# Low parts of weight pieces by GpSimd's accumulating DMA in an encoder's mixers

## The chip, the cores and the metric

The kernel runs on one core of a Trainium2 chip. The metric is the device time of one execution in microseconds (us); the median of three runs of the kernel before is 834.88 us (833.3 to 836.93). Five engines run side by side, each in the order of its own instructions: TensorE (PE) multiplies, VectorE (DVE) and ScalarE (ACT) work on tiles, GpSimd (POOL) does small work, and SyncE (SP) issues DMA transfers. They wait for each other by semaphores.

## The reference

Two layers of an encoder block for 256 tokens of 1,024 float32 values. In each layer, three branches (mLSTM, Fourier, S5) are computed from one projection, gated and summed, and a squared-ReLU MLP follows:

```python
for l in range(DEPTH):
    h = rmsnorm(x, g_mix_pre[l])
    z = h @ w_in[l] + b_in[l]                       # q, k, v, o, gates of the cells, Fourier, S5, 3 x 1024 gates
    y_m = mlstm_branch(z[q, k, v, o, ig, fg]) @ w_up_mlstm[l]
    y_f = fourier_branch(z[fourier]) @ w_up_fourier[l]
    y_s = s5_branch(z[s5], ...)
    gates = sigmoid(z[gates])
    mixed = gates[0] * y_m + gates[1] * y_f + gates[2] * y_s
    x = x + rmsnorm(mixed @ w_out[l], g_mix_post[l])
    f = square(relu(rmsnorm(x, g_ffn_pre[l]) @ w_ffn1[l])) @ w_ffn2[l]
    x = x + rmsnorm(f, g_ffn_post[l])
```

## The kernel before

Every large product is made in three matmuls of a shorter float format (float32r). A weight W and the activations h are each split into a high and a low part, and PE adds hi·hi, hi·lo and lo·hi into a PSUM bank (`mm3`, lines 261 to 264). The split of the activations, `hhi` and `hlo`, is done once per layer.

The weights come in pieces. A piece of the mixers' pairs is 512 rows by 256 columns of the weight (512 KB), as a tile of 128 partitions by 4 row blocks by 256 columns. `wload` (lines 190 to 205) makes it ready in three steps: SP loads `raw` from device memory (L200), ACT rounds it to `hi` (tile `whi`, L202), and DVE subtracts, lo = raw - hi (tile `wlo`, L204). There are 5 raw tiles, 4 `whi` and 4 `wlo` tiles; a step waits until the tile that it writes is free.

`wstat_pair` (lines 323 to 335) makes 256 output columns for all tokens as two halves of one PSUM bank. It takes two pieces one after the other, and for each piece 2 halves x 4 row blocks x 3 = 24 matmuls of 256 columns, with the weights as the stationary operand. ACT then evicts the two halves, to the q and k tile `qk` (L1043) or through a tanh for the gates (L1062). In one mixer the pairs come in this order: one for S5, four for q and k, two for the output gate o, four for branch gate 1 and four for gate 2; the four of gate 0 come later, among the up-projections.

Between the pieces, `tick(budget)` takes steps from two side queues, in which the convolutions, the mLSTM cells, the Fourier branch and the S5 branch are written as generators. What finally sets the order on each engine is a list scheduler that plays the program through with costs of its own when it is built; the kernel gives it the program order, the buffers and a few fixed orders. So an edit in one place can move instructions elsewhere.

Two side steps matter below. The stabilisers of the cells (`stabilisers`) write a small tile to device memory (`md`), read it back as a broadcast of 1,024 KB into the ring tile `Gm` (L856, by SP), and then POOL runs four selects on it (L870). The ring tile is free only after PE has read the S5 tables that lay in it (L685). And at the end of the mixer, `cell_norm` (POOL L957 and L958, ACT L964) scales the heads `hm`, `cell_out` transposes them on PE (L188, tiles acc from hm), and DVE and ACT make the operand `ym` (L974, L976) of the mLSTM up-projection.

POOL issues no DMA in this kernel.

Of the kernel before, what the change touches and what calls it, by code (L numbers as in the profile page):

```python
# [10 lines left out]
F32 = mybir.dt.float32  # L11
F32R = mybir.dt.float32r
AF = mybir.ActivationFunctionType
ALU = mybir.AluOpType

P = 128
D = 1024
# [3 lines left out]
NK = D // P  # L21
# [12 lines left out]
OFF_Q = 0  # L34
# [6 lines left out]
OFF_GATE = OFF_S5 + M_S5  # L41
# [77 lines left out]
def encoder_kernel(ctx: ExitStack, tc: tile.TileContext, a: dict, out: bass.AP):  # L119
# [67 lines left out]
    def transpose(o, i, k=P):  # L187
        nc.tensor.transpose(o, i, cst[:k, C_ID:C_ID + k])  # L188

    def wload(pieces, shape, in_ring=None):  # L190

        raw = wp.tile(shape, F32, tag="raw", name=nm("raw"))
        if in_ring:
            both = ring(in_ring, [P, 2] + shape[1:], F32R)
            hi, lo = both[:, 0], both[:, 1]
        else:
            hi = wp.tile(shape, F32R, tag="whi", name=nm("whi"), bufs=TAIL)
            lo = wp.tile(shape, F32R, tag="wlo", name=nm("wlo"), bufs=TAIL)
        for dst, src in pieces:
            nc.sync.dma_start(dst(raw), src)  # L200
        yield
        act(hi, raw, AF.Copy)  # L202
        yield
        latest[0] = V.tensor_sub(lo, raw, hi.bitcast(F32)).ins  # L204
        return hi, lo
# [7 lines left out]
    def pieces_of(w, k0, kn, c0, cn):  # L213
        return ([(lambda r: r, w[k0 * P:(k0 + kn) * P, c0:c0 + cn].rearrange("(k p) c -> p k c", p=P))], [P, kn, cn])

    def now(gen):

        while True:
            try:
                next(gen)  # L220
            except StopIteration as e:
                return e.value
# [29 lines left out]
            while self.at[2] < len(self.specs):  # L252
                self.lo()

    def wunit(pieces, shape, in_ring=None):
        return now(wload(pieces, shape, in_ring))

    def wcols(w, k0, kn, c0, cn, in_ring=None):
        return wunit(*pieces_of(w, k0, kn, c0, cn), in_ring)

    def mm3(o, lhi, llo, rhi, rlo, start, stop):
        mm(o, lhi, rhi, start=start, stop=False)  # L262
        mm(o, lhi, rlo, start=False, stop=False)  # L263
        mm(o, llo, rhi, start=False, stop=stop)  # L264
# [55 lines left out]
        while side[which]:  # L320
            tick(1.0)

    def wstat_pair(w, c0, nk, ahi, alo, kper=4, budget=0.0):


        bank = mm_ps()
        ps = [bank[:, c * S:(c + 1) * S] for c in range(2)]
        for k0 in range(0, nk, kper):
            hi, lo = wcols(w, k0, kper, c0, 2 * P)
            for c in range(2):  # L330
                for k in range(kper):
                    mm3(ps[c], hi[:, k, c * P:(c + 1) * P], lo[:, k, c * P:(c + 1) * P],
                        ahi[:, k0 + k, :], alo[:, k0 + k, :], k0 + k + c == 0, k0 + k + c == nk)
            tick(budget)
        return bank

    def rstd_of(ss):
# [654 lines left out]
    def mixer(l, iu, vu, after):  # L992
# [44 lines left out]
            side[1].append(s5_branch(l, U, yg))  # L1037
        side[0] += [stabilisers(l, zf, st), fourier(zf, fo_y)][::-1 if l == 0 else 1]
        for nq, c2 in enumerate((1, 3, 0, 2)):
            ps = wstat_pair(w, OFF_Q + c2 * 2 * P, NK, hhi, hlo, budget=B)  # L1040
            for c in range(2):
                i = c2 * 2 + c
                act(qk[:, i, :], ps[:, c * S:(c + 1) * S], AF.Identity, bias=col(l, "qkb", i))  # L1043
                side[0].append(conv_silu(l, qk, i))
            if nq % 2:
                for h in range(2 * (c2 % 2), 2 * (c2 % 2) + 2):
                    side[0].append(cells(l, qk, st, h))
# [8 lines left out]


        def gate_pair(g, c2, dst, budget):
            ps = wstat_pair(w, OFF_GATE + g * D + c2 * 2 * P, NK, hhi, hlo, budget=budget)
            for c in range(2):  # L1060
                i = c2 * 2 + c
                act(dst(i), ps[:, c * S:(c + 1) * S], AF.Tanh, scale=0.5, bias=col(l, "gb", g * 8 + i, half=True))  # L1062
# [281 lines left out]
```

## Time and profile before

| | |
|---|---|
| median of three runs | 834.88 us (833.3 to 836.93) |
| the profiled execution | 834.29 us, its span 831.6 us |
| PE busy | 810.7 us (97%) |
| DVE busy | 597.6 us (72%) |
| ACT busy | 472.4 us (57%) |
| POOL busy | 30.3 us (4%) |
| DMA | 147.87 MB, 178 GB/s in the mean; one hardware queue holds nearly all of it |

The profile is of one execution. Its span goes from the first to the last instruction; the execution's time is 2.7 us more. Busy time of PE counts a matmul as long as it is in the array, and matmuls overlap, so the distance of two starts says more than a duration. An engine's idle time costs only where another engine is waiting for it.

### The profile page before, as it was taken

How to read it: one execution, taken by the hardware profiler on the slowest of the kernel's cores; microseconds unless marked ns; L12 is line 12 of the kernel's file. 1: busy time of each engine (PE TensorE's matmuls, PEld its weight loads, DVE VectorE, ACT ScalarE, POOL GpSimd, SP SyncE). 2: the span in 40 equal slices, each digit the busy share in tenths (PEclk: the TensorE clock that was granted, in tenths of full speed). 3: DMA queues.
4: the chain of work that ended last, by engine and by line, in shares of the span. 5: the costliest groups of instructions: out<-in, count | busy, mean ns of one | idle time of the engine just before them, and what ended most of it. 6: DMA issues, size and time to landing. Idle time of an engine off the chain costs nothing.

```text
span 831.6 us, 14910 instructions
## 1 busy us (share of the span) xinstructions
PE 810.7 (97%) x5825; PEld 749.4 (90%) x5825; DVE 597.6 (72%) x1071; ACT 472.4 (57%) x784; POOL 30.3 (4%) x51
## 2 busy tenths in 40 slices
PE   7999999998999999999999999999999999999996
PEld 5899999998878999999879999999997899999995
DVE  5898899887685567667568798776876755555563
ACT  4668764586464458467654355666865444444451
POOL 1000200000020000000010010000000100000000
PEclk9999999999999999999999999999999999999999
DMA  8785843554755564765837554555666555566651
GB/s 264 222 229 142 247 121 103 152 177 148 257 138 179 185 188 137 235 186 186 271 96 229 152 179 128 152 178 153 176 185 215 181 158 193 185 186 195 181 174 50
DMA packets 122262, 147.87 MB, mean 178 GB/s; under 512 B 22310, under 2 KB 104398, under 8 KB 121936
## 3 DMA queue, kind: packets, MB, share of 16 engines
q1 hardware_dynamic: 122044, 146.66, 57.9%
q8 instruction: 45, 0.74, 0.4%
q10 hardware_dynamic: 148, 0.27, 0.1%
q14 instruction: 25, 0.20, 0.1%
HBM read 144.33 MB, written 2.57 MB: 177 GB/s over the span
## 4 chain that ended last, share of the span: by engine, by line
PE 71%; DVE 2%; ACT 1%; issue 1%; POOL 1%; DVEq 0%; POOLq 0%; ACTq 0%
PE mm L262 12%; PE mm L264 12%; PE mm L263 12%; PE acc L263 8%; PE acc L264 8%; PE acc L262 8%; PE mm L279 2%; PE mm L278 2%; PE mm L295 1%; PE mm L188 1%; PE mm L281 1%; PE acc L743 1%; PE acc L939 1%; DVE wlo L204 1%; DVE x_sb L386 0%
## 5 line engine op out<-in xcount | busy, mean ns | idle before, releaser
L204 DVE TENSOR_TENSOR wlo<-raw,whi 128x1024 fp32r<-128x1024 f32 (+1 forms) x237 | 287.6, 1215 | 153.1 <-ACT whi L202 152.1
L202 ACT ACTIVATE whi<-raw 128x1024 fp32r<-128x1024 f32 (+1 forms) x237 | 248.5, 1052 | 241.3 <-PE mm L263 141.6
L262 PE MATMUL mm<-hT,whi 128*128 128x256 f32 x1024 | 290.9, 284 | 0.0
L264 PE MATMUL mm<-hT,wlo 128*128 128x256 f32 x1024 | 290.4, 284 | 0.0
L263 PE MATMUL mm<-hT,whi 128*128 128x256 f32 x1024 | 290.2, 283 | 0.0
L262 PEld LDWEIGHTS mm<-hT,whi 128*128 128x128 f32 x1024 | 192.8, 188 | 1.5
L263 PEld LDWEIGHTS mm<-hT,whi 128*128 128x128 f32 x1024 | 192.9, 188 | 1.1
L264 PEld LDWEIGHTS mm<-hT,wlo 128*128 128x128 f32 x1024 | 193.3, 189 | 0.2
L263 PE MATMUL acc<-wlo,ringB 128*128 128x512 f32 x280 | 109.3, 392 | 0.7 <-DVE wlo L204 0.7
L264 PE MATMUL acc<-whi,ringB 128*128 128x512 f32 x280 | 108.8, 391 | 0.0
L262 PE MATMUL acc<-whi,ringB 128*128 128x512 f32 x280 | 106.2, 390 | 0.0
L263 PEld LDWEIGHTS acc<-wlo,ringB 128*128 128x128 f32 x280 | 52.6, 188 | 12.1 <-DVE wlo L204 1.9
L264 PEld LDWEIGHTS acc<-whi,ringB 128*128 128x128 f32 x280 | 52.6, 188 | 11.0
L262 PEld LDWEIGHTS acc<-whi,ringB 128*128 128x128 f32 x280 | 52.6, 188 | 10.2
L279 PE MATMUL mm<-whi,hT 128*128 128x512 f32 (+1 forms) x84 | 30.3, 369 | 1.9 <-DVE hT L371 1.8
L906 DVE SCALAR_TENSOR_TENSOR t1k<-ringB,pc,t1k 128x254 f32<-128x254 f32 (+1 forms) x64 | 31.0, 484 | 0.9
L278 PE MATMUL mm<-whi,hT 128*128 128x512 f32 (+1 forms) x84 | 30.5, 373 | 0.7 <-ACT whi L202 0.5
L262 PE MATMUL mm<-ringB,whi 128*128 128x256 f32 x96 | 27.4, 286 | 1.7 <-ACT ringB L976 1.7
L380 DVE SCALAR_TENSOR_TENSOR w2k<-acc,ringA 128x512 f32<-128x512 f32 x16 | 10.6, 688 | 24.7 <-ACT t1k L378 24.7
L263 PE MATMUL mm<-ringB,whi 128*128 128x256 f32 x96 | 27.3, 285 | 0.0
L264 PE MATMUL mm<-ringB,wlo 128*128 128x256 f32 x96 | 27.2, 284 | 0.0
L378 ACT ACTIVATE t1k<-acc 128x512 bf16<-128x512 f32 x16 | 9.5, 595 | 30.4 <-PE acc L264 30.4
(334 smaller groups left out, 1156.8 us busy)
## 6 DMA issues: line engine op xcount, KB each, us to landing
raw<-in_w_ffn_dram SPq DMA_DIRECT2D x128, 512.0 KB
raw<-in_w_in_dram SPq DMA_DIRECT2D x84, 512.0 KB
raw<-in_w_out_dram SPq DMA_DIRECT2D x16, 512.0 KB
raw<-in_w_glu_dram SPq DMA_DIRECT2D x16, 256.0 KB
raw<-in_w_up_mlstm_dram SPq DMA_DIRECT2D x8, 512.0 KB
ringB<-md SPq DMA_DIRECT2D x2, 1024.0 KB
raw<-in_w_up_fourier_dram SPq DMA_DIRECT2D x4, 512.0 KB
raw<-in_w_in_dram SPq DMA_DIRECT2D x4, 408.0 KB
```

The source lines that it names most:

```text
L188: nc.tensor.transpose(o, i, cst[:k, C_ID:C_ID + k])
L202: act(hi, raw, AF.Copy)
L204: latest[0] = V.tensor_sub(lo, raw, hi.bitcast(F32)).ins
L262: mm(o, lhi, rhi, start=start, stop=False)
L263: mm(o, lhi, rlo, start=False, stop=False)
L264: mm(o, llo, rhi, start=False, stop=stop)
L278: mm(o, hhi[:, k, tt], hi, start=k == 0, stop=False)
L279: mm(o, hlo[:, k, tt], hi, start=False, stop=False)
L281: mm(o, hhi[:, k, tt], lo, start=False, stop=k == NK - 1)
L378: act(junk(), ps[c], AF.Square, accum_out=ss[:, c:c + 1])
L380: stt(f, ps[c], ROOT_D, gpost[:, half(c)], ALU.mult, ALU.mult)
L906: stt(u[:, lo_:hi_], z[:, lo_ + o:hi_ + o], col(l, "cw", j * 8 + i), u[:, lo_:hi_], ALU.mult, ALU.add)
```

## The change

In the q and k pairs and in the pairs of gates 1 and 2, the low part of the second of the two pieces is made in another way: ACT writes lo = -hi (the rounding of raw with a scale of -1), and a DMA that POOL issues adds raw to it in place. The products with this low part are taken out of their triples and put at the end of the pair, after the `tick`. The S5 and o pairs, gate 0 and everything else keep the subtraction. It touches 4 + 8 pairs per layer, 24 in all.

```diff
-    def wload(pieces, shape, in_ring=None):
+    def wload(pieces, shape, in_ring=None, by_dma=False):
...
         yield
         act(hi, raw, AF.Copy)
+        if by_dma:
+            act(lo, raw, AF.Copy, scale=-1.0)
+            yield
+            G.dma_start(lo.bitcast(F32), raw, accum_op=ALU.add)
+            return hi, lo
         yield
         latest[0] = V.tensor_sub(lo, raw, hi.bitcast(F32)).ins
...
-    def wstat_pair(w, c0, nk, ahi, alo, kper=4, budget=0.0):
+    def wstat_pair(w, c0, nk, ahi, alo, kper=4, budget=0.0, by_dma=False):
...
+        late = []
         for k0 in range(0, nk, kper):
-            hi, lo = wcols(w, k0, kper, c0, 2 * P)
+            dma = by_dma and k0 + kper == nk
+            hi, lo = wcols(w, k0, kper, c0, 2 * P, by_dma=dma)
             for c in range(2):
                 for k in range(kper):
-                    mm3(ps[c], hi[:, k, c * P:(c + 1) * P], lo[:, k, c * P:(c + 1) * P],
-                        ahi[:, k0 + k, :], alo[:, k0 + k, :], k0 + k + c == 0, k0 + k + c == nk)
+                    cs = slice(c * P, (c + 1) * P)
+                    if dma:
+                        mm(ps[c], hi[:, k, cs], ahi[:, k0 + k, :], start=False, stop=False)
+                        mm(ps[c], hi[:, k, cs], alo[:, k0 + k, :], start=False, stop=False)
+                        late.append((ps[c], lo[:, k, cs], ahi[:, k0 + k, :], k0 + k + c == nk))
+                    else:
+                        mm3(ps[c], hi[:, k, cs], lo[:, k, cs], ahi[:, k0 + k, :], alo[:, k0 + k, :],
+                            k0 + k + c == 0, k0 + k + c == nk)
             tick(budget)
+        for o, w_, x, stop in late:
+            mm(o, w_, x, start=False, stop=stop)
         return bank
...
-            ps = wstat_pair(w, OFF_Q + c2 * 2 * P, NK, hhi, hlo, budget=B)
+            ps = wstat_pair(w, OFF_Q + c2 * 2 * P, NK, hhi, hlo, budget=B, by_dma=True)
...
-            ps = wstat_pair(w, OFF_GATE + g * D + c2 * 2 * P, NK, hhi, hlo, budget=budget)
+            ps = wstat_pair(w, OFF_GATE + g * D + c2 * 2 * P, NK, hhi, hlo, budget=budget, by_dma=g > 0)
```

The scheduler orders the changed program anew. Three places follow; the numbers in a tile's name differ between the two programs, and lines behind the edit are higher by 5 to 16.

PE in layer 1, the end of the first pair of gate 2 and the start of the next pair. `hT_84` and `hT_85` are the high and low activations, `mm_...` the pair's bank. Before:

```order
L262 MATMUL mm_6496<-hT_84,whi_6528 128x256
L263 MATMUL mm_6496<-hT_85,whi_6528 128x256
L264 MATMUL mm_6496<-hT_84,wlo_6529 128x256
L262 MATMUL mm_6559<-hT_84,whi_6561 128x256
L263 MATMUL mm_6559<-hT_85,whi_6561 128x256
```

And now:

```order
L342 MATMUL mm_6516<-hT_84,whi_6548 128x256
L343 MATMUL mm_6516<-hT_85,whi_6548 128x256
L350 MATMUL mm_6516<-hT_84,wlo_6549 128x256 x8
L268 MATMUL mm_6580<-hT_84,whi_6582 128x256
L269 MATMUL mm_6580<-hT_85,whi_6582 128x256
```

The eight products with the low part stand together, directly behind the sixteen with the high part, and the next pair follows them.

POOL in layer 0, from the norm before the mixer (`rs`) to the norm of the cells (`rsd`). Before:

```order
L340 TENSOR_SCALAR rs_26_153<-ss_148 128x1
L342 TENSOR_TENSOR rs_27_155<-rs_26_153,mhalf 128x1
L870 AFFINE_SELECT ringB_734<-ringB_734 128x4x128
L870 AFFINE_SELECT gx_945<-ringB_734 128x512
L870 AFFINE_SELECT gx_946<-ringB_734 128x512
L870 AFFINE_SELECT ringB_734<-ringB_734 128x4x128
L957 TENSOR_SCALAR rsd_1488<-mv_1090 128x8
```

And now, from the DMA of the last q and k pair (`wlo_1215`) over that of the first gate pair (`wlo_1566`) on:

```order
L207 DMA wlo_1215<-raw_1213 128x1024
L207 DMA wlo_1566<-raw_1564 128x1024
L886 AFFINE_SELECT ringB_734<-ringB_734 128x4x128
L886 AFFINE_SELECT gx_946<-ringB_734 128x512
L886 AFFINE_SELECT gx_947<-ringB_734 128x512
L886 AFFINE_SELECT ringB_734<-ringB_734 128x4x128
L207 DMA wlo_1663<-raw_1661 128x1024
L207 DMA wlo_1771<-raw_1769 128x1024
```

POOL had nothing but the selects between its two norms; now it has five of layer 0's twelve DMAs ahead of the four selects and seven behind them; `wlo_1663`, of the second gate pair, is the first behind.

PE at the end of layer 0's mixer, the transposes of the heads `hm`. Before, behind the third gate 0 pair (`mm_2581`):

```order
L264 MATMUL mm_2581<-hT_84,wlo_2614 128x256
L188 MATMUL acc_2220<-cst,hm_1088 128x128
L188 MATMUL acc_2220<-cst,hm_1089 128x128
L188 MATMUL acc_2227<-cst,hm_1088 128x128
L188 MATMUL acc_2227<-cst,hm_1089 128x128
L188 MATMUL acc_2234<-cst,hm_1088 128x128
L188 MATMUL acc_2234<-cst,hm_1089 128x128
L188 MATMUL acc_2241<-cst,hm_1088 128x128
L188 MATMUL acc_2241<-cst,hm_1089 128x128
L262 MATMUL mm_2650<-ringB_2185,whi_2645 128x256
```

And now, inside the S5 up-projection (`mm_2513`, `mm_2514`, whose operand is `yg`):

```order
L270 MATMUL mm_2513<-yg_94,wlo_2508 128x256
L188 MATMUL acc_2232<-cst,hm_1083 128x128
L188 MATMUL acc_2232<-cst,hm_1084 128x128
L188 MATMUL acc_2239<-cst,hm_1083 128x128
L188 MATMUL acc_2239<-cst,hm_1084 128x128
L188 MATMUL acc_2246<-cst,hm_1083 128x128
L188 MATMUL acc_2246<-cst,hm_1084 128x128
L268 MATMUL mm_2514<-yg_94,whi_2507 128x256
```

Six of the eight transposes moved ahead of three blocks of the S5 up-projection and of the whole gate pair; the last two stand one block later. The products that read `ym` (before `mm_2650<-ringB_2185`) still come after the gate pair.

## Rows read from the trace of the kernel before

**Rows 1.** The page's shares of the span, all engines: busy us (share) xinstructions.

```profile
PE 810.7 (97%) x5825; PEld 749.4 (90%) x5825; DVE 597.6 (72%) x1071; ACT 472.4 (57%) x784; POOL 30.3 (4%) x51
```

**Rows 2.** Order of time on PE, layer 1: start, duration, operation.

```profile
504.36 0.28 PE L262 MATMUL mm<-hT,whi 128*128 128x256 f32 x1
504.48 0.28 PE L263 MATMUL mm<-hT,whi 128*128 128x256 f32 x1
```

**Rows 3.** Stretches: length, busy PE, PEld, DVE, ACT, POOL; clock, DMA share, GB/s.

```profile
40.00:200.00 160.00, 157.38 (x1417) 155.21 (x1416) 141.53 (x342) 109.00 (x217) 8.46 (x6) 1.00 0.56 163
...
60.00:80.00 20.00, 20.00 (x167) 19.61 (x166) 17.88 (x42) 17.71 (x36) 0.00 (x0) 1.00 0.58 148
80.00:100.00 20.00, 20.00 (x225) 19.72 (x224) 18.28 (x24) 15.52 (x31) 5.42 (x4) 1.00 0.81 240
180.00:200.00 20.00, 17.63 (x145) 17.08 (x144) 15.76 (x30) 14.15 (x31) 3.04 (x2) 1.00 0.42 132
530.00:550.00 20.00, 20.00 (x169) 20.00 (x169) 15.16 (x32) 12.60 (x23) 0.00 (x0) 1.00 0.57 162
```

**Rows 4.** Groups of instructions: shapes xcount | busy us, mean ns | idle before.

```profile
L204 DVE TENSOR_TENSOR wlo<-raw,whi 128x1024 fp32r<-128x1024 f32 (+1 forms) x237 | 287.6, 1215 | 153.1 <-ACT whi L202 152.1
L202 ACT ACTIVATE whi<-raw 128x1024 fp32r<-128x1024 f32 (+1 forms) x237 | 248.5, 1052 | 241.3 <-PE mm L263 141.6
```

**Rows 5.** Order of time on ACT, layer 1's gates; [idle before, releaser].

```profile
543.01 1.06 ACT L202 ACTIVATE whi<-raw 128x1024 fp32r<-128x1024 f32 x1 [0.97 <-PE mm L263]
543.98 0.82 ACT L1062 ACTIVATE ringA<-mm,pch 128x256 f32<-128x256 f32 x2
```

**Rows 6.** Order of time on SP's queue: broadcasts, and loads of layer 1.

```profile
86.75 0.34 SPq L856 DMA_DIRECT2D ringB<-md  x1
...
437.59 10.08 SPq L200 DMA_DIRECT2D raw<-in_w_in_dram  x8
...
488.24 0.34 SPq L856 DMA_DIRECT2D ringB<-md  x1
```

**Rows 7.** Order of time on ACT, the first load of that stretch.

```profile
441.44 1.06 ACT L202 ACTIVATE whi<-raw 128x1024 fp32r<-128x1024 f32 x1 [2.02 <-DMA raw<-in_w_in_dram]
```

**Rows 8.** Order of time on PE, layer 0, the last read of the old ring tile.

```profile
86.37 0.31 PE L685 MATMUL acc<-Wt,ringB 128*32 128x32 f32 x16
```

**Rows 9.** Order of time on POOL: first and last select, layers 0 and 1.

```profile
94.35 1.50 POOL L870 TENSOR_SCALAR_AFFINE_SELECT ringB<-ringB 128x512 f32<-128x512 f32 x1 [82.92 <-DMA raw<-in_w_in_dram]
...
98.15 1.61 POOL L870 TENSOR_SCALAR_AFFINE_SELECT ringB<-ringB 128x512 f32<-128x512 f32 x1
...
492.58 0.95 POOL L870 TENSOR_SCALAR_AFFINE_SELECT ringB<-ringB 128x512 f32<-128x512 f32 x1 [59.74 <-DMA ringB<-md]
...
494.67 0.63 POOL L870 TENSOR_SCALAR_AFFINE_SELECT ringB<-ringB 128x512 f32<-128x512 f32 x1
```

**Rows 10.** One stretch of layer 0's q and k, columns as in rows 3.

```profile
36.75:63.09 26.34, 26.34 (x220) 26.19 (x219) 26.29 (x88) 17.28 (x28) 0.00 (x0) 1.00 0.79 220
```

**Rows 11.** ACT's roundings in that stretch, as a group.

```profile
L202 ACT ACTIVATE whi<-raw 128x1024 fp32r<-128x1024 f32 x8 | 8.5, 1057 | 8.2 <-PE mm L263 8.2
```

**Rows 12.** Order of time on ACT, four activations for S5's tables.

```profile
68.45 1.69 ACT L661 ACTIVATE Wt<-ringA,cst 128x256 f32<-128x256 f32 x4
```

**Rows 13.** Order of time on PE, last cell products to the mLSTM branch's products.

```profile
177.69 0.72 PE L939 MATMUL acc<-v_sb,t1k 128*128 128x129 f32 x5
...
191.30 0.79 PE L188 MATMUL acc<-cst,hm 128*128 128x128 f32 x4 [0.63 <-DVE t1k L974]
193.83 0.39 PE L262 MATMUL mm<-ringB,whi 128*128 128x256 f32 x1 [1.74 <-ACT ringB L976]
```

**Rows 14.** Order of time on DVE in that chain; each kind comes again.

```profile
179.83 1.23 DVE L204 TENSOR_TENSOR wlo<-raw,whi 128x1024 fp32r<-128x1024 f32 x1 [0.62 <-ACT whi L202]
180.98 0.68 DVE L1120 SCALAR_TENSOR_TENSOR w2k<-w2k,w2k 128x512 f32<-128x512 f32 x1
```

**Rows 15.** Order of time on ACT, the scalings of the heads.

```profile
188.52 3.20 ACT L964 ACTIVATE hm<-hm,nb,rsd 128x128 f32<-128x128 f32 x8 [0.19 <-DVE nb L960]
```

More of the change, by code (lines that the diff above doesn't have):

```diff
@@ L253, in all, with wunit, wcols @@
                 self.lo()
[L255 to L259, printed above, removed]
+    def wunit(pieces, shape, in_ring=None, by_dma=False):
+        return now(wload(pieces, shape, in_ring, by_dma))
+    def wcols(w, k0, kn, c0, cn, in_ring=None, by_dma=False):
+        return wunit(*pieces_of(w, k0, kn, c0, cn), in_ring, by_dma)
     def mm3(o, lhi, llo, rhi, rlo, start, stop):
```

## The prediction

> **What bounds the kernel.** I read the shares of the span first: TensorE (PE) is busy 810.7 of 831.6 us, VectorE (DVE) 72%, ScalarE (ACT) 57%, GpSimd (POOL) 4% [rows 1]. A busy PE need not be a full one, so the second view is the order of time on PE inside a product pair: a 256-column matmul starts every 0.12 us, without a hole [rows 2]. The stretches then say how long that lasts: of 40 to 200 us, layer 0's mixer, PE idles 2.6 us (157.38 of 160.00), and 2.37 of these lie between 180 and 200; from 530 to 550, in layer 1's gates, it makes 169 matmuls in 20 us, 0.12 us each [rows 3]. So the stretches that the change edits run at PE's rate already, and what can be won there is what PE idles: 2.6 us in layer 0. The granted clock is 1.00 (2.4 GHz) in each of these rows, the one with the 2.37 us idle too; I carry no term for it.
>
> **The change, term by term.**
> *Work removed and added.* Of 237 low parts of this form 24 leave DVE: 4 q and k pairs and 8 gate pairs in each of two layers. That is 24 x 1.215 = 29.2 us of DVE, and 24 negations at ACT's 1.052 us for the same shape, 25.2 us of ACT [rows 4]. PE makes the same matmuls. As PE is the bound, neither counts by itself.
>
> *The new wait.* PE is in order: behind the first late product everything on PE waits, then ACT's roundings, then SP's loads. How much cover has the DMA? There are four hi buffers: ACT starts a rounding when PE is done with the piece four back, as at 543.01 [rows 5]. At that moment three pieces of 24 x 0.12 = 2.88 us lie ahead, 8.64 us; the piece four back now still owes its own 8 late products (0.96), and this piece's 16 hi products come first (1.92): 11.52 us. From it go ACT's rounding 1.06, the two evictions of an earlier pair that now stand between (0.82) [rows 5], and the negation 1.06. So 8.6 us are left between the end of the negation and the first late product where pairs follow without other PE work, and more elsewhere.
>
> The trace has no DMA of POOL and no accumulating one. Bounds from the nearest rows: a 512 KB load was issued at 437.59, and the rounding that waited for it began at 441.44: 3.85 us [rows 6, 7]. The 1,024 KB broadcast of the stabilisers took 4.34 us in layer 1 (488.24 to the first select at 492.58) and 7.60 us in layer 0 (86.75 to 94.35) [rows 6, 9]. An accumulate of 512 KB has to read two such tiles, the bytes of the broadcast, so I put it between 4.34 and 7.60, at the middle, 6.0, since the DMA share of the stretches is 0.57 to 0.81 [rows 3]. That is below 8.6, even at 7.60: cost 0 where POOL's queue is free. By the Trainium skill, DMA: Bandwidth & Descriptors, section on the anatomy of a GpSimd DMA, such a transfer takes about 2.0 us plus its bytes over 436 GB/s, an estimate of 3.2 us here; by it this term and the stall below would both be 0. No row here shows a GpSimd DMA.
>
> *Buffers and traffic.* The raw tile is now freed when the DMA lands, some 0.82 + 1.06 + 6.0 - 1.2 = 6.7 us later. There are five raw tiles, so a load is issued about 5 x 2.88 - 1.2 = 13.2 us before its rounding and needs 3.85: slack 9.3 us, cost 0. On the DMA engines one load per 2.88 us makes a share of 0.57 in layer 1's gates; one accumulate for two loads adds half of that if it costs like a load, all of it if it costs double: 0.86 to 1.14. Above 1 the 46 us of eight gate pairs would stretch by 0.14 x 46 = 6.4 us; I take 0.86, nothing.
>
> *The queue on POOL.* In layer 0 the DMA of the second gate pair now stands behind four selects, which wait for the broadcast. SP issued that at 86.75, as PE ended its last read of the old ring tile (86.37 + 0.31) [rows 6, 8]. In the new order PE has from there to the first late product of that pair 110 matmuls of 0.12, 13.2 us, and some 18 small ones, 1.5: 14.7 us. In that time must fit the broadcast (4.34 to 7.60), the selects (2.72 in layer 1, 492.58 to 495.30, and 5.41 in layer 0, 94.35 to 99.76) [rows 9], and the DMA (3.85 to 7.60): 10.9 to 20.6 us. The stall is 0 to 5.9; at the middles, 5.97 + 4.07 + 5.7 = 15.7, it is 1.0 us, which I take. In layer 1 the selects stand before the gates, with two output pairs between: 0.
>
> *ACT in layer 0's q and k.* From 36.75 to 63.09, 26.34 us, ACT is busy 17.28 and idles 9.1, 8.2 of it for PE [rows 10, 11]. The new order puts into the same stretch 3 negations (3.2 us), 16 table activations pulled forward (0.42 each by the row of four [rows 12], 6.8 us) and one more (0.6): 27.9 us. So ACT falls back at least 1.6 us, and 10.7 if all of the idle time came again. Its lead is 8.64 - 1.06 = 7.6 us. PE would lose 0 to 3.1 us; a late ACT doesn't wait for PE, so I take 1.6 + 0.9 = 2.5, below the lead: 0.
>
> *The gap at the end.* The 2.37 us are 0.63 before the second four transposes and 1.74 before the products of the mLSTM branch [rows 13]. The chain there runs from the last cell products, which PE leaves at about 178.2, over DVE and POOL's norm to eight scalings, ended 191.72: 13.5 us [rows 13, 15]; PE had 99 matmuls, 11.9 us, in between. In the new order six of the transposes stand 80 matmuls (9.6 us) behind that product, and PE needs their results only 84 products later. DVE's part of the chain loses what lay in it: two subtractions of 1.2 and three operations of 0.68 [rows 14], 4.5 us. So the chain is 9.0 to 13.5 us against 9.6: a wait of 0 to 3.9 where 2.37 was; I take 0.4, a gain of 2.0.
>
> Sum on the profiled execution: 834.29 - 2.0 + 1.0 = 833.3. It lies 0.6 below the median of 834.88, so the forecast for the median is 834, no change; its own range is 831 to 838 (the three runs spread by 3.6). About 0.5%, 4.2 us, is what a measurement of this kernel tells from none.
>
> **Rivals.**
> *A, slower: the DMA is later than its cover.* For it: POOL's time hangs on what DVE does beside it. With DVE's two-input table products the selects of layer 0 took 1.50 to 1.61 us, the last of layer 1 took 0.63 [rows 9]. If the DMA's time grows as the select's did, by 2.5, 4.34 becomes 10.9 us. It decides from 8.6 us on: 2.3 us for each of some 14 pairs that follow closely (4 q and k and 3 gates in layer 0, 7 gates in layer 1), 32 us, and some 5 more at the selects: 834.9 - 2 + 37 = 870. Against: that is nearly three times what a plain load takes. The Trainium skill, SBUF — State Buffer, section on the two separate sides, names such a trap: while DVE holds the port pair that it shares with GpSimd, GpSimd can't write its DMA's descriptors; further on, under who interferes with whom, it takes two-input operations, DVE's main work here, out of that, as an inference. The selects' times agree that the two engines share something; a delayed descriptor is in no row.
>
> *B, slower: the second gate pair.* The broadcast at 7.60 and the selects at 5.41, as in layer 0 before, and a DMA at 7.60: stall 5.9, with the gap only kept: 834.9 + 5.9 = 841, and 844 with ACT's 3.1. It decides where broadcast, selects and DMA together pass 14.7 + 4.2. For: the DMA share is 0.81 from 80 to 100. Against: the broadcast is issued some 9 us earlier now, towards a stretch with 0.58 [rows 3].
>
> *C, faster: DVE is the true bound where it is full.* From 36.75 to 63.09 it is busy 26.29 of 26.34 [rows 10]. If PE were paced by it, the three subtractions taken out here, and generously as many in the gates, would give 6 x 1.215 = 7.3 us: 827.6. Against: PE's 220 matmuls of 0.12 fill the same 26.34 us.
>
> **Numbers.** Forecast 0.57, A 0.16, B 0.19, C 0.08. So faster 0.08, same 0.57, slower 0.16 + 0.19 = 0.35. The range leaves out A and C: 831 (all of the idle 2.6 won, and the spread of the runs) to 846 (5.9 + 3.1 + the 1.5 by which the gap may grow).
>
> **What would show it.** Right: no wait in front of the late products, the second gate pair of layer 0 aside; DVE's subtraction 213 times for 237 with PE's busy time unchanged; the gap near 190 under 1 us. Wrong: PE rows that wait for a DMA in most pairs, a landing over 8.6 us after the negation (A); PE idle over 4 us between 90 and 100 behind POOL's selects (B); a stall in front of the six transposes, where my chain was too short.

## The result, and the profile after

| | median us | runs |
|---|---|---|
| before | 834.88 | 833.30 to 836.93, 3 runs |
| changed | 844.34 | 843.97 to 846.46, 3 runs |

The ratio is 1.0111, with an interval of 1.0077 to 1.0144: 9.5 us slower. The forecast was no change. The profiled execution of the changed kernel took 846.46 us, 12.2 more than that of before. Its page, in the columns of [rows 1], and the queue that POOL's DMAs use (packets, MB, share of 16 engines' span):

```profile
PE 817.8 (97%) x5825; PEld 756.6 (90%) x5825; DVE 572.2 (68%) x1047; ACT 494.3 (59%) x808; POOL 50.4 (6%) x75
...
q1 hardware_dynamic: 122044, 146.66, 56.7%
q0 software_dynamic: 3456, 12.58, 8.1%
```

In the page's totals DVE lost 25.4 us and ACT took 21.9; by the groups below it is 29.2 (287.6 to 258.4) and 25.3, as counted. PE makes the same 5,825 matmuls, but is busy 7.1 us longer: its mean granted clock is 0.988, for 0.998 before. The groups that answer to [rows 4], and the new DMA with its time to landing:

```profile
L210 DVE TENSOR_TENSOR wlo<-raw,whi 128x1024 fp32r<-128x1024 f32 (+1 forms) x213 | 258.4, 1216 | 170.1 <-ACT whi L203 169.0
L205 ACT ACTIVATE wlo<-raw 128x1024 fp32r<-128x1024 f32 x24 | 25.3, 1056 | 0.0
...
wlo<-raw POOLq DMA_DIRECT2D x24, 512.0 KB, 6.0
```

The DMA lands after 6.0 us in the median, which is what I had taken (4.5 to 10.1 over the 24). PE's waits, as a list (total us, times, longest):

```profile
PE acc L188 <- DVE t1k L868: 4.3, 1, 4.3
...
PE mm L350 <- DMA wlo<-raw: 3.5, 3, 1.9
...
PE acc L188 <- DVE t1k L990: 0.4, 1, 0.4
```

Only three of 24 pairs wait for their DMA. The longest new wait is for another thing: the stabilisers' tile from DVE (`t1k`, L868). The stretches, as in [rows 3], say where:

```profile
60.00:80.00 20.00, 14.66 (x101) 14.26 (x100) 12.88 (x35) 15.92 (x33) 0.00 (x0) 0.83 0.77 194
100.00:120.00 20.00, 18.10 (x189) 17.49 (x189) 7.12 (x17) 15.53 (x33) 1.89 (x3) 0.91 1.04 247
180.00:200.00 20.00, 19.61 (x167) 19.41 (x166) 15.20 (x33) 17.25 (x38) 1.86 (x2) 1.00 0.53 160
```

From 60 to 80 us PE makes 101 matmuls where it made 167. The gap near 190 is gone: 19.61 us busy for 17.63.

To add this up, I take the same work on PE (counted in streamed columns) in both traces and ask how much later it starts. Change of that lag in us, by stretches of the trace of before, for the profiled executions of the changed kernel and of the experiments told below. Runs of one kernel can lie 13 us apart with their mean clock (e2_qk: 837.0 us at 0.996, 850.2 at 0.982), and each row is one execution set against one of before, 834.29 us, so a sum is not the ratio of the medians.

| kernel | 0-60 | 60-90 | 90-122 | 122-186 | 186-198 | 198-end | sum |
|---|---|---|---|---|---|---|---|
| changed | -0.1 | +7.8 | +4.0 | +0.7 | -3.4 | +3.1 | +12.1 |
| e1_gates | -0.1 | 0.0 | +6.1 | +0.7 | -3.3 | 0.0 | +3.4 |
| e2_qk | +0.9 | +5.8 | +0.3 | -0.3 | -3.3 | +0.2 | +3.6 |
| e4_small | -0.3 | -0.3 | +0.5 | +0.3 | -3.4 | 0.0 | -3.2 |
| e6_l1 | -0.2 | 0.0 | 0.0 | 0.0 | +2.7 | +0.8 | +3.3 |
| e3_late | +1.0 | -0.3 | +0.6 | +0.6 | -2.8 | +3.1 | +2.1 |
| e9_pool | +6.5 | +0.1 | +1.6 | +4.9 | -3.4 | +6.0 | +15.7 |
| e12_copy | +1.2 | +3.6 | +0.3 | +0.3 | -3.4 | +3.0 | +4.9 |
| e13_hi | +1.5 | +1.6 | +4.7 | +0.3 | -3.4 | +0.8 | +5.5 |
| e14_g2l0 | +0.2 | 0.0 | +1.4 | +0.7 | -3.3 | 0.0 | -1.0 |
| e17_noqk3 | +0.2 | +3.4 | +1.6 | -0.2 | -3.4 | +1.1 | +2.7 |
| e18_nosel2 | -0.2 | +7.6 | +0.3 | +1.8 | -3.4 | +1.7 | +7.8 |
| e21_acttab | -0.1 | +9.8 | +2.2 | +0.4 | -3.4 | +0.7 | +9.5 |

**60 to 90 us, +7.8.** PE's order of time in the changed kernel (columns as in [rows 5]):

```profile
66.38 0.38 PE L350 MATMUL mm<-hT,wlo 128*128 128x256 f32 x1 [1.07 <-DMA wlo<-raw]
71.03 0.35 PE L188 MATMUL acc<-cst,t1k 8*128 8x8 f32 x2 [4.27 <-DVE t1k L868]
```

DVE's, where it waits, and then the same operations in the trace of before (L864 is L848 there, L577 is L561):

```profile
67.98 0.29 DVE L577 TENSOR_TENSOR ringA<-par,ringA 128x128 f32<-128x128 f32 x1 [6.98 <-DMA ringA<-in_s_b_re_dram]
68.19 0.67 DVE L864 TENSOR_TENSOR_SCAN t1k<-cst,t1k 8x256 f32<-8x256 f32 x1
...
70.42 0.47 DVE L868 SCALAR_TENSOR_TENSOR t1k<-t1k,cst,t1k 8x256 f32<-8x256 f32 x1
```

```profile
63.98 0.67 DVE L848 TENSOR_TENSOR_SCAN t1k<-cst,t1k 8x256 f32<-8x256 f32 x1
...
65.54 0.27 DVE L561 TENSOR_TENSOR ringA<-par,ringA 128x128 f32<-128x128 f32 x1
```

And SP's queue, in the changed kernel and then before:

```profile
33.01 12.47 SPq L201 DMA_DIRECT2D raw<-in_w_in_dram  x5
45.53 1.10 SPq L736 DMA_DIRECT2D zd<-zsT  x1
52.49 2.05 SPq L739 DMA_DIRECT2D U<-zd  x4
54.65 2.32 SPq L201 DMA_DIRECT2D raw<-in_w_in_dram  x4
57.02 5.03 SPq L604 DMA_DIRECT2D ringA<-in_s_b_re_dram  x2
```

```profile
42.31 0.50 SPq L720 DMA_DIRECT2D zd<-zsT  x1
...
48.07 1.82 SPq L723 DMA_DIRECT2D U<-zd  x4
49.99 8.50 SPq L200 DMA_DIRECT2D raw<-in_w_in_dram  x5
58.54 2.05 SPq L588 DMA_DIRECT2D ringA<-in_s_b_re_dram  x2
```

Read it from the end. PE has two transposes of the stabilisers' tile (L188) standing between the late products of the fourth q and k pair. The tile comes from DVE, where the stabilisers' scans (L864) stand behind one small operation on the S5 tables (L577). That one waits 7 us for its two loads, which SP issued from 57.02 on: 11.0 us. In the trace of before the scans stood ahead of it, and the same loads, issued from 58.54 on, were there when DVE came to them at 65.54: 7.0 us at most. So a load that the change doesn't touch is late, and DVE's queue hands its lateness to PE. Behind each of the two long waits the clock falls (stretches of the changed kernel, columns as in [rows 3]):

```profile
72.00:77.00 5.00, 5.00 (x26) 5.00 (x25) 4.93 (x18) 2.44 (x7) 0.00 (x0) 0.53 0.82 252
...
104.00:108.00 4.00, 4.00 (x24) 4.00 (x23) 2.12 (x6) 4.00 (x8) 0.00 (x0) 0.57 1.05 251
```

At 0.53, nearly all of it at the level of 1.2 GHz, PE makes 26 matmuls in 5 us; before it made 41 in that stretch at 1.00.

**90 to 122 us, +4.0.** SP's broadcast, to be read beside [rows 6], and POOL's queue, beside [rows 9]:

```profile
85.77 0.34 SPq L872 DMA_DIRECT2D ringB<-md  x1
```

```profile
92.56 3.56 POOL L886 TENSOR_SCALAR_AFFINE_SELECT ringB<-ringB 128x512 f32<-128x512 f32 x1 [7.21 <-DMA ringB<-md]
96.09 1.58 POOL L886 TENSOR_SCALAR_AFFINE_SELECT gx<-ringB 128x512 f32<-128x512 f32 x2
97.62 0.81 POOL L886 TENSOR_SCALAR_AFFINE_SELECT ringB<-ringB 128x512 f32<-128x512 f32 x1
98.39 1.75 POOL L207 DMA_DIRECT2D wlo<-raw  x2
```

The second gate pair's DMA leaves at 98.39 behind the selects, and PE, in a hole of 1.90 us, gets its data at 103.03; the lower clock follows again.

**198 us to the end, +3.1.** Most of it is clock at the lower level: once behind a short wait at the norm near 438 us, which was there before at 1.00, and once from 479.5 to 483 us with PE busy throughout. The third wait for a DMA is here, at 553.9 us, 0.5 us.

### The profile page after: what moved, and what is told of

The parts are those of the page before. It is cut to its first block, busy times and chain, and to the rows that moved or that the text cites. A ratio compares the mean times of both kernels' runs of the same rounds, so it can differ in the third digit from the quotient of the medians.

```text
span 843.7 us, 14966 instructions
## 1 busy us (share of the span) xinstructions
PE 817.8 (97%) x5825; PEld 756.6 (90%) x5825; DVE 572.2 (68%) x1047; ACT 494.3 (59%) x808; POOL 50.4 (6%) x75
## 3 DMA queue, kind: packets, MB, share of 16 engines
q1 hardware_dynamic: 122044, 146.66, 56.7%
## 4 chain that ended last, share of the span: by engine, by line
PE 82%; DVE 6%; DMA 5%; issue 2%; ACT 2%; POOL 1%; SPq 0%; POOLq 0%; DVEq 0%; ACTq 0%
PE mm L268 13%; PE mm L269 13%; PE mm L270 12%; PE acc L269 8%; PE acc L270 8%; PE acc L268 8%; PE mm L350 2%; PE mm L285 2%; PE mm L284 2%; PE mm L343 2%; PE mm L342 2%; DVE wlo L210 2%; PE acc L759 2%; DMA wlo<-raw 2%; PE acc L188 1%
## 5 line engine op out<-in xcount | busy, mean ns | idle before, releaser
L210 DVE TENSOR_TENSOR wlo<-raw,whi 128x1024 fp32r<-128x1024 f32 (+1 forms) x213 | 258.4, 1216 | 170.1 <-ACT whi L203 169.0
L268 PE MATMUL mm<-hT,whi 128*128 128x256 f32 x832 | 237.7, 286 | 0.0
L269 PE MATMUL mm<-hT,whi 128*128 128x256 f32 x832 | 237.1, 285 | 0.0
L270 PE MATMUL mm<-hT,wlo 128*128 128x256 f32 x832 | 237.0, 285 | 0.0
L270 PEld LDWEIGHTS mm<-hT,wlo 128*128 128x128 f32 x832 | 158.5, 191 | 0.2
L269 PEld LDWEIGHTS acc<-wlo,ringB 128*128 128x128 f32 x280 | 52.6, 188 | 12.1 <-DVE wlo L210 2.0
L342 PE MATMUL mm<-hT,whi 128*128 128x256 f32 x192 | 48.5, 287 | 0.0
L343 PE MATMUL mm<-hT,whi 128*128 128x256 f32 x192 | 48.3, 286 | 0.0
L356 POOL TENSOR_SCALAR rs<-ss 128x1 f32<-128x1 f32 x16 | 7.8, 486 | 499.2 <-DVE w2k L396 348.5
L350 PE MATMUL mm<-hT,wlo 128*128 128x256 f32 x192 | 31.1, 301 | 3.5 <-DMA wlo<-raw 3.5
L207 POOL DMA_DIRECT2D wlo<-raw x24 | 21.2, 894 | 204.0 <-ACT wlo L205 116.0
L285 PE MATMUL mm<-whi,hT 128*128 128x512 f32 (+1 forms) x84 | 31.4, 380 | 1.9 <-DVE hT L387 1.8
```

The costliest lines, as they stand in the source:

```text
L207: G.dma_start(lo.bitcast(F32), raw, accum_op=ALU.add)
L285: mm(o, hlo[:, k, tt], hi, start=False, stop=False)
L342: mm(ps[c], hi[:, k, cs], ahi[:, k0 + k, :], start=False, stop=False)
L343: mm(ps[c], hi[:, k, cs], alo[:, k0 + k, :], start=False, stop=False)
L350: mm(o, w_, x, start=False, stop=stop)
```

## The experiments

Theory T: the accumulates' bytes and their landing make the loss, through the queues of SP, DVE and POOL. The rivals are in the expectations. Ratios are to the kernel before, run beside each; its median was 836.5 to 836.8 us in these comparisons.

**e4_small: the bytes taken away.** Order of layer 0 unchanged.

```diff
-            G.dma_start(lo.bitcast(F32), raw, accum_op=ALU.add)
+            G.dma_start(lo.bitcast(F32)[:, 0:1, 0:16], raw[:, 0:1, 0:16], accum_op=ALU.add)
```

> As the changed kernel, but each accumulating DMA moves 16 columns of one row block, 8 KB for 512 KB, so the low parts lack most of raw (the output isn't the reference's); layer 0's order is the changed kernel's. It takes away the DMA's bytes and time and leaves the order, the negations and the late products. Theory T (traffic): the table loads are late since the accumulates fill the DMA engines (share 1.03 from 58 to 64 us against 0.83 before); without them the tables are there when VectorE asks, at 61 us, PE has no wait in the last q and k pair, and the second gate pair waits less than 0.5 us: 829 to 834 us. Rival O (order alone): the loads are issued at 57.0 and take the 7.0 us that they took at most before, until 64.0; with the 3.0 us from there to the stabilisers' tile PE still waits until 67.0, 1.9 us in place of 5.6, at full clock or with some low clock behind: 835 to 838 us.

830.79 us, ratio 0.9932 (0.9916 to 0.9948): theory T, not the order alone. DVE and SP in the same place:

```profile
60.33 0.29 DVE L577 TENSOR_TENSOR ringA<-par,ringA 128x128 f32<-128x128 f32 x1 [0.33 <-DMA ringA<-in_s_b_re_dram]
```

```profile
42.59 1.60 SPq L736 DMA_DIRECT2D zd<-zsT  x1
48.33 1.83 SPq L739 DMA_DIRECT2D U<-zd  x4
50.27 4.94 SPq L201 DMA_DIRECT2D raw<-in_w_in_dram  x4
55.26 1.05 SPq L604 DMA_DIRECT2D ringA<-in_s_b_re_dram  x2
```

The table's first two loads are there 5.1 us after the first issue, and DVE waits 0.33 us in the same order of instructions. Negations, late products and order together are even a gain. Its profile shows 3.2 us of that; its runs have mean clocks of 0.997 to 0.999, those of the kernel before 0.992 to 0.998.

**e1_gates and e2_qk: one half each.**

```diff
-            ps = wstat_pair(w, OFF_Q + c2 * 2 * P, NK, hhi, hlo, budget=B, by_dma=True)
+            ps = wstat_pair(w, OFF_Q + c2 * 2 * P, NK, hhi, hlo, budget=B)
```
```diff
-            ps = wstat_pair(w, OFF_GATE + g * D + c2 * 2 * P, NK, hhi, hlo, budget=budget, by_dma=g > 0)
+            ps = wstat_pair(w, OFF_GATE + g * D + c2 * 2 * P, NK, hhi, hlo, budget=budget)
```

> The DMA only in the pairs of gates 1 and 2 (16 of 24); the q and k pairs keep the subtraction. Theory P (three places): of the changed kernel's delay, 8.9 us arise in layer 0's last q and k pair, where VectorE waits 7.0 us for a load of the S5 tables with the stabilisers' scans queued behind it; in this kernel's order the scans stand ahead of the tables again, so PE has no hole from 60 to 80 us and the time is 834 to 840 us, what is left being the second gate pair of layer 0 (4.5) and layer 1. Rival D (every DMA costs a bit, by ACT's negation and the longer life of the raw tiles): two thirds of 9.5, 841 us, with PE's loss spread over the gate pairs.

> The DMA only in the q and k pairs (8 of 24); the gates keep the subtraction. Layer 0's order up to the output gate's pairs is word for word that of the changed kernel. Theory P: the wait of 4.3 us for the stabilisers' tile and the low clock behind it stay, 8.9 us, and the selects' stall is gone: 841 to 846 us. Rival D: a third of 9.5: 838 us.

e1_gates 837.48 us, 1.0018 (1.0005 to 1.0032); e2_qk 839.50 us, 1.0043 (1.0010 to 1.0076). By the table the two losses part as P said: 60 to 90 us belongs to q and k alone (0.0 against 5.8), 90 to 122 to the gates alone (6.1 against 0.3). In e1_gates one of PE's two waits for a DMA, 2.1 us, is not for one behind the selects, but for one that POOL issued ahead of them, at 86.25, and that landed 9.2 us later. e2_qk (837.04 to 850.17) ended below its range: its wait for the tile was 3.5 us, and the gain at 186 to 198, which each half brings whole, I had left out of the sum. Its trace is that of its fastest execution and doesn't show what made three of the ten take over 848.

**e6_l1: layer 1 alone.**

```diff
-            ps = wstat_pair(w, OFF_Q + c2 * 2 * P, NK, hhi, hlo, budget=B, by_dma=True)
+            ps = wstat_pair(w, OFF_Q + c2 * 2 * P, NK, hhi, hlo, budget=B, by_dma=l > 0)
...
-            ps = wstat_pair(w, OFF_GATE + g * D + c2 * 2 * P, NK, hhi, hlo, budget=budget, by_dma=g > 0)
+            ps = wstat_pair(w, OFF_GATE + g * D + c2 * 2 * P, NK, hhi, hlo, budget=budget, by_dma=g > 0 and l > 0)
```

> The DMA only in layer 1 (12 of 24); layer 0 is the kernel before, word for word. Theory P: layer 1 carries 2 to 3 us of the delay, from the low clock at 480 to 485 us behind a run of small products and 0.7 us of waits for the DMA; 835 to 838 us. Rival D: half of 9.5, 840 us.

839.83 us (836.50 to 846.22), 1.0051 (1.0023 to 1.0078): the 840 of rival D, but inconclusive. In the profiled execution, of 836.81 us, no product of layer 1 waits for a DMA, and the lag from 198 us on is 0.8. What it shows instead lies in the untouched layer 0, the old gap near 190:

```profile
180.00:200.00 20.00, 17.62 (x122) 17.07 (x122) 14.96 (x29) 13.27 (x29) 3.05 (x2) 0.83 0.44 132
```

The same 2.4 us of idle time as in [rows 3], there at 1.00 and 145 matmuls, here with the clock at 0.83 behind it and 122. So the old gap can cost 2.7 us more than the trace of before shows, in code that the change doesn't touch. The spread of 10 us over the runs of e6_l1, at mean clocks of 0.994 down to 0.986, isn't explained by this one trace.

**e12_copy: what the addition costs.** Instruction for instruction the changed kernel.

```diff
-            G.dma_start(lo.bitcast(F32), raw, accum_op=ALU.add)
+            G.dma_start(lo.bitcast(F32), raw)
```

> As the changed kernel, instruction by instruction, but the DMA only copies raw over the low part and adds nothing (the low part is then all of raw, so the output isn't the reference's). It prices the addition. If a DMA's bytes set its time, all stays: 2.85 us of all 16 engines for each of the 24 transfers, 6.0 us to landing, the wait of some 4 us in layer 0's last q and k pair, 841 to 846 us. If the addition costs, the copy needs what a load does, 1.7 us of the engines and 4 to 5 us to landing, the wait shrinks to 0 to 2 us: 833 to 839 us.

836.69 us, 1.0007 (0.9989 to 1.0026). The same packets and bytes:

```profile
q0 software_dynamic: 3456, 12.58, 3.9%
...
wlo<-raw POOLq DMA_DIRECT2D x24, 512.0 KB, 4.1
```

Of 16 engines a copy takes 0.039 x 836.6 / 24 = 1.36 us, an accumulate 0.081 x 843.7 / 24 = 2.85 us, a weight load 0.567 x 843.7 x 0.524 / 146.66 = 1.71 us. The addition doubles the engines' time and adds 1.9 us to the landing; it makes most of the loss, and PE waits for none of the copies, only for the stabilisers' tile, 2.4 us. It doesn't make all of the tables' delay: issued from 56.13 on, they are there at 66.10, still 10.0 us later.

**e13_hi: raw freed early, same bytes.** The low parts of the 24 pieces are left out.

```diff
-            G.dma_start(lo.bitcast(F32), raw, accum_op=ALU.add)
+            G.dma_start(lo.bitcast(F32), hi.bitcast(F32), accum_op=ALU.add)
```

> As the changed kernel, but the DMA adds the high part in place of raw (the low part becomes zero, so the output isn't the reference's): the same bytes, but raw is free once ScalarE has read it, so SyncE's loads don't wait for the DMA. Layer 0's order up to the selects is the changed kernel's but for one load. Theory T: the traffic stays and so does the wait in layer 0's last q and k pair, 3 to 5 us, 840 to 845 us. Rival R (it is the raw tile's longer life, through SyncE's queue): the load held by the first DMA is issued 3 us earlier, and with it the S5 input and the tables behind it on SyncE; they are there by 63 us, PE waits 0 to 1 us: 833 to 838 us.

842.79 us (838.19 to 850.63; the trace is of 839.17), 1.0081 (1.0047 to 1.0115): the total goes with T, the place with R. SP is held no longer:

```profile
32.92 8.46 SPq L201 DMA_DIRECT2D raw<-in_w_in_dram  x5
41.70 0.59 SPq L736 DMA_DIRECT2D zd<-zsT  x1
42.56 0.37 SPq L201 DMA_DIRECT2D raw<-in_w_in_dram  x1
51.34 3.04 SPq L739 DMA_DIRECT2D U<-zd  x4
54.48 1.69 SPq L201 DMA_DIRECT2D raw<-in_w_in_dram  x3
56.22 1.39 SPq L604 DMA_DIRECT2D ringA<-in_s_b_re_dram  x2
```

`zd` leaves 3.8 us earlier than in the changed kernel, but takes 9.6 us to where `U` can follow. Only three loads, not four, stand right ahead of the tables, which then need 6.7 us, and the wait for the stabilisers' tile is 1.0 us. The rest has moved: the accumulates land after 7.5 us in the median (5.1 to 11.2), and PE waits 4.5 us for three of them.

**e17_noqk3 and e18_nosel2: single accumulates left out.**

```diff
-            ps = wstat_pair(w, OFF_Q + c2 * 2 * P, NK, hhi, hlo, budget=B, by_dma=True)
+            ps = wstat_pair(w, OFF_Q + c2 * 2 * P, NK, hhi, hlo, budget=B, by_dma=l > 0 or nq < 3)
```
```diff
-            ps = wstat_pair(w, OFF_GATE + g * D + c2 * 2 * P, NK, hhi, hlo, budget=budget, by_dma=g > 0)
+            ps = wstat_pair(w, OFF_GATE + g * D + c2 * 2 * P, NK, hhi, hlo, budget=budget, by_dma=g > 0 and (l > 0 or g > 1 or c2 > 1))
```

> As the changed kernel without the accumulate of layer 0's fourth q and k pair, the one issued at 56.27 that landed 10.1 us later, 23 of 24. VectorE still has the S5 table's operation ahead of the scans, and PE's transposes of the stabilisers' tile stand some 3.5 us later. If that one transfer is what delays the tables (2.85 us of all 16 engines), the tile comes 2.9 us earlier and PE waits 0 to 1 us there: of the 8.9 us 6 to 9 are gone, ratio to before 1.001 to 1.005. If the delay was collected before it, by the earlier loads and the S5 input (its load landed 4.4 us later than without bytes), the tables stay late, by 65 to 68 us, PE waits 1 to 3 us, ratio 1.004 to 1.010.

> As the changed kernel without the accumulates of layer 0's first two gate 1 pairs (22 of 24): none stands right ahead of the selects or right behind them. By the stretches, the second gate pair's wait of 2.05 us with the low clock behind it made 4.3 to 5 us of the loss: these go and the rest stays, ratio to before 1.003 to 1.007. Rival: the loss at 96 to 110 us is not that DMA's wait but the traffic of the region, and it turns up at the third pair: ratio 1.008 to 1.011.

e17_noqk3 837.05 us, 1.0018 (1.0000 to 1.0036): without one of 24 transfers most of the loss is gone. The first two table loads, issued from 57.27 on, are there at 65.13, 7.9 us later, and PE waits 0.6 us for the tile. From 60 to 90 us 3.4 of the 7.8 stay, in waits of 1.1 us for an ACT operation on the tables (L677) and of 1.0 for another pair's DMA above all. e18_nosel2 842.06 us, 1.0072 (1.0043 to 1.0101): the loss at 90 to 122 us goes (+0.3), that at 60 to 90 stays (+7.6). The ratio of e18_nosel2 lies between the two forecasts; it is the table that tells them apart. So both places answer to the transfers concerned, though each edit also has the scheduler reorder what follows (e17_noqk3 has 1.6 for 4.0 at 90 to 122).

**e21_acttab: the tables by another queue.**

```diff
-                    nc.sync.dma_start(crow[:, i, :, dup, :], src)
+                    (nc.scalar if l == 0 and b else nc.sync).dma_start(crow[:, i, :, dup, :], src)
```

The loads into `braw` likewise.

> As the changed kernel, all 24 accumulates, but the S5 table loads of layer 0's second block (eight small loads) are issued by ScalarE, not by SyncE behind four weight loads and the S5 input. If SyncE's order is what makes them late (each of its loads also waits for a semaphore of one eight before), they are issued by 54 us, there by 60, and PE has no wait at the stabilisers' tile: ratio 1.000 to 1.004. If the full DMA engines make them late, they take 10 us and more from any queue, VectorE waits as long, and PE with it: ratio 1.006 to 1.012.

843.48 us, 1.0120 (1.0074 to 1.0166). The time doesn't decide between the two: ACT's own work stands still for 9.2 us behind the issues of these loads, and PE waits 4.1 us for ACT (L677) and only 0.8 for the stabilisers' tile.

```profile
65.15 0.91 ACT L677 ACTIVATE ringA<-ringA,cst 128x256 f32<-128x256 f32 x2 [9.23 <-DMA ringA<-in_s_b_re_dram]
```

What decides is the landing, and it goes with the full engines, not with SP's order. ACT issued the first table loads from 55.52 on, and DVE had them at 67.72:

```profile
67.72 0.29 DVE L577 TENSOR_TENSOR ringA<-par,ringA 128x128 f32<-128x128 f32 x1 [9.22 <-DMA ringA<-in_s_b_re_dram]
```

12.2 us, though nothing of SP stood ahead of them on ACT's queue. The Trainium skill, DMA: Bandwidth & Descriptors, section "Issuing engines are not separate DMA queues", says that DMAs which ScalarE, SyncE or GpSimd start all run on the same 16 DMA engines. This run agrees: 12.2 us from ACT's queue, 11.0 from SP's.

**e3_late: the order of the products alone.**

```diff
-            act(lo, raw, AF.Copy, scale=-1.0)
             yield
-            G.dma_start(lo.bitcast(F32), raw, accum_op=ALU.add)
+            latest[0] = V.tensor_sub(lo, raw, hi.bitcast(F32)).ins
```

> Only the order of the products: the low part's products last, its subtraction on VectorE as before, no negation and no DMA. It parts the gain of the kernel with 8 KB transfers (ratio 0.9932) between the late products and the relief of VectorE. If the relief of VectorE (29 us) makes it, this is as before, 834 to 838 us in the measure of the last comparison, ratio 0.998 to 1.002; if the late products make it, by their longer cover, 830 to 833 us, ratio 0.992 to 0.996.

835.08 us, 0.9984 (0.9973 to 0.9996): between the two, nearer to none. So the late products are not what costs. And the gap near 190 is gone here too:

```profile
180.00:200.00 20.00, 20.00 (x168) 19.84 (x168) 17.59 (x33) 16.24 (x34) 3.04 (x2) 1.00 0.54 161
```

DVE makes all 237 subtractions in this kernel and no DMA is added, so the 2.8 us won at 186 to 198, of the changed kernel's 3.4, come with the order of the instructions alone.

**e9_pool: no DMA, GpSimd subtracts.**

```diff
-            act(lo, raw, AF.Copy, scale=-1.0)
             yield
-            G.dma_start(lo.bitcast(F32), raw, accum_op=ALU.add)
+            G.tensor_sub(lo, raw, hi.bitcast(F32))
```

> The 24 low parts by a subtraction on GpSimd's own ALU: no negation on ScalarE, no DMA, products last as in the changed kernel. Theory T (the accumulates' traffic and landing are the cause): without their bytes this runs as the kernel with 8 KB transfers did, 829 to 833 us (ratio to before 0.991 to 0.996), since GpSimd's 1,024 columns, by its selects of 512 columns at 0.63 to 1.78 us, take 1.3 to 3.6 us of the 8.6 us of cover. Rival S (GpSimd and VectorE hold each other up): VectorE's operations beside it are lengthened, the subtraction's 1.216 us to 1.6 or more, and PE waits for VectorE: 836 to 842 us.

850.82 us, 1.0175 (1.0157 to 1.0192): theory T alone would have made this fast; rival S holds, but not by a longer subtraction on DVE (1,227 ns in the mean). Beside 20 of POOL's 24 subtractions one operation of DVE, whichever it is, takes 1.2 to 2.6 us and ends with POOL's or at most 0.6 us behind it; together they take 38 us more than such operations take in the changed kernel, and most others beside them keep their time. The operation in the second line takes 0.17 us there:

```profile
40.87 2.88 POOL L206 TENSOR_TENSOR wlo<-raw,whi 128x1024 fp32r<-128x1024 f32 x1 [0.80 <-ACT whi L203]
```

```profile
41.44 2.34 DVE L463 TENSOR_TENSOR ey<-ey,ab 128x16 f32<-128x16 f32 x1
```

It often falls on the convolutions' taps, whose mean rises by it. In e9_pool, then in the changed kernel:

```profile
L921 DVE SCALAR_TENSOR_TENSOR t1k<-ringB,pc,t1k 128x255 f32<-128x255 f32 x32 | 24.1, 752 | 0.7
```

```profile
L922 DVE SCALAR_TENSOR_TENSOR t1k<-ringB,pc,t1k 128x255 f32<-128x255 f32 x32 | 15.8, 495 | 0.6
```

PE's new waits in this trace are 6.6 us for DVE, 2.6 for ACT and 1.2 for POOL; that each goes back to such an operation is likely, but not traced one by one. POOL needs 2.82 us in the mean, 2.36 at least, where DVE needs 1.22. That agrees with the Trainium skill, GPSIMD Engine Reference, section "Engine selection", which puts two-input element work there at about half of VectorE's speed. The expectation's 1.78 us as the longest select was too low: one takes 3.56 in the changed kernel.

**e14_g2l0: the accumulate only where there is room.**

```diff
-            ps = wstat_pair(w, OFF_Q + c2 * 2 * P, NK, hhi, hlo, budget=B, by_dma=True)
+            ps = wstat_pair(w, OFF_Q + c2 * 2 * P, NK, hhi, hlo, budget=B)
...
-            ps = wstat_pair(w, OFF_GATE + g * D + c2 * 2 * P, NK, hhi, hlo, budget=budget, by_dma=g > 0)
+            ps = wstat_pair(w, OFF_GATE + g * D + c2 * 2 * P, NK, hhi, hlo, budget=budget, by_dma=g > 1 and l == 0)
```

> The DMA only in the four pairs of gate 2 in layer 0 (4 of 24), the stretch of 120 to 160 us in which the DMA engines' share is 0.40 without it and VectorE is full. The order of the last transposes at 190 us is the spread one of the other variants. Theory T: the transfers find room here, nothing waits, and what is left is the gain at 190 us that every variant had, 3.2 to 3.3 us: 832 to 834 us in the measure of the comparisons so far (before 836.5), ratio 0.994 to 0.998. Rival D (each accumulate costs wherever it stands, a twenty-fourth of the loss, 0.5 us): the gain is eaten to 1 us, ratio 0.998 to 1.001.

833.34 us, 0.9971 (0.9955 to 0.9987): faster than both. From 120 to 160 us, before and then here:

```profile
120.00:160.00 40.00, 40.00 (x336) 39.79 (x336) 37.94 (x90) 18.23 (x33) 0.00 (x0) 1.00 0.39 113
```

```profile
120.00:160.00 40.00, 40.00 (x340) 39.89 (x339) 38.65 (x99) 20.94 (x36) 1.74 (x2) 1.00 0.56 153
```

Two of the four accumulates leave in this stretch, at 129.3 and 135.8, and two ahead of it, at 105.8 and 111.3, where 100 to 120 us had 0.48 before. The share rises from 0.39 to 0.56, no late product waits, and the gain at 186 to 198 us stays. That gain is one of order, as e3_late shows. What e14_g2l0 adds is that no transfer is waited for here. The 1.4 lost at 90 to 122 is a wait of 1.5 us, at 109 us, for ACT (L688), which now has a negation of 1.05 us ahead of that operation. The interval reaches the 0.998 of rival D, so the place of the loss speaks against D more than the time does.

## Why the prediction was wrong

*Work removed and added: right.* 213 subtractions, 24 negations, and no loss from either in the changed kernel (in e14_g2l0 one negation costs a wait of 1.5 us).

*The new wait: right in the mean, wrong in the tail.* 6.0 us to landing was measured, and 21 of 24 pairs don't wait. The estimate of 3.2 us set beside it lies under every one of the 24 landings, 4.5 at least. Those that land late are the ones issued into full engines: 10.1 us at 56.27, where the share is 1.03 (58 to 64 us), and 8.7 at 108.4, where it is 1.02 (108 to 117).

*Buffers and traffic: this step failed,* with its "cost 0" for the raw tile and its "I take 0.86, nothing". Three things were wrong in it. The cost of an accumulate was taken as a load's; it is 1.67 loads (2.85 against 1.71 us). The share was worked out for layer 1's gates, from 0.57, and not for layer 0's q and k, which had 0.79 in [rows 10] and have 0.95 in the same stretch of the changed kernel. And only the weight loads' slack was looked at, not what else uses SP and the DMA engines there. The raw tile that is freed late doesn't stall its rounding; it holds SP, so that `zd` leaves at 45.53 for 42.31 before, its transfer to the load of `U` takes 7.0 us for 5.8, and four loads of 1.71 us leave together at 54.65 (five went out over 8.5 us before), with an accumulate of 2.85 at 56.27. The tables come behind these 9.7 us of work and need 11.0. Without that accumulate they need 7.9 (e17_noqk3), with one load fewer ahead 6.7 (e13_hi), without bytes 5.1 (e4_small). That the engines' time is not the whole price shows in e12_copy, where a copy of 1.36 us stands there and they need 10.0. I had the load of the tables in none of my rows.

*A term that was missing: DVE's queue.* I read the new order for POOL and PE, not for DVE, where the table operation had moved ahead of the scans. The order alone costs nothing (e4_small); with the late load it costs PE 4.3 us. PE's wait for the accumulate itself is 1.1 us, and the low clock behind the two makes most of the rest of the 7.8.

*The queue on POOL: the mechanism right, the term mis-sized.* Broadcast 6.8 us (85.77 to 92.56), selects 5.8, DMA 4.6: 17.3, against 15.4 until PE got there; I had 15.7 against 14.7. The wait is 1.9 us for 1.0, and 4.0 with the clock. The selects were slower than in either layer before (5.83 against 5.41): one took 3.56 us. The broadcast, forecast some 9 us earlier than before, left only 1.0 us earlier, since PE had lost 7.8 us by then; in e4_small it left at 77.51, 9.2 us earlier.

*ACT in layer 0's q and k: right,* no wait for a rounding there.

*The gap at the end: right in size; of the two causes given, the order does most.* 2.0 us of idle time were forecast to go and 0.4 to stay; PE's busy time from 180 to 200 us rose by 1.98, to 19.61, and 0.4 stayed. With the order alone and no relief of DVE 2.8 of the lag's 3.4 go (e3_late). (The lag falls by more than 2.0, since some small products also stand elsewhere in the order.)

*The clock: "I carry no term for it" was wrong.* Behind the new waits it fell; the three runs have mean clocks of 0.988 to 0.993, for 0.998 in the profiled run of before (0.992 to 0.998 in the runs of before beside the experiments).

Of the rivals, B gave the right time (841 to 844), but its mechanism is a third of the loss (e18_nosel2); that 844.34 lies inside the range of 831 to 846, whose top is B's, is luck. A's landing over 8.6 us happened twice, not in most pairs.

What stays open is layer 1: e6_l1 is 0.5% slower, with a wide spread, and its trace shows no wait that the change could have made. Rival D, a small cost of every accumulate, has e1_gates against it (837.48 for its 841), but nothing rules it out for layer 1 alone.

## What to carry to other kernels

A transfer that is hidden for its own consumer can still delay the other transfers of its stretch: add its engine time to the share there, and follow the small loads that are issued into the same stretch to whoever waits for them. When an edit makes a scheduler reorder, read the new order of every engine on which a wait can be handed on, not only of those that the edit touches. Move work to DMA where the share is low: twenty-four accumulates lost 1.1%, and four where the share was 0.39 to 0.48 were never waited for. And before a gain is credited to the work that was moved, run the new order without the move: here the order alone (e3_late) made most of the gain at 190 us.

## What was not expected of the hardware

- An accumulating DMA between SBUF tiles takes 2.85 us of all 16 engines for 512 KB and 6.0 us to land, a plain copy of the same packets 1.36 and 4.1, and POOL is busy 0.87 us to issue the one, 0.53 the other.
- An 8 KB accumulate took 2.1 to 8.1 us to land, 2.6 in the median (e4_small); the one of 8.1 left at 77.0 us, just ahead of SP's 1,024 KB broadcast (77.51).
- Beside 20 of 24 subtractions on POOL one operation of DVE was held to 1.2 to 2.6 us, one of 16 columns to 2.34 for 0.17; most others kept their time (e9_pool).
- From 479.5 to 483 us of the changed kernel the clock was at the lower level with PE busy without a hole; ahead of it, from 474.8 us on, stood 32 products of 64 columns and then a group of products of 4 columns. Behind the same two groups it fell in e12_copy (471.6 us) and in e9_pool, which has no accumulating DMA (479.5), but not in e6_l1, e17_noqk3, e18_nosel2 and e21_acttab.
